# New places for the background pieces among TensorE's products in a two-layer hybrid decoder

## The chip, the cores and the metric

The kernel runs on one core of a Trainium2 chip. The metric is the device time of one execution in microseconds (us), the median of several runs. Five engines work side by side, each through its own instructions in their order: TensorE (PE; its weight loads are listed apart as PEld), VectorE (DVE), ScalarE (ACT), GpSimd (POOL) and SyncE (SP), which issues most of the DMA transfers. A result of one engine that another needs is passed on by a semaphore, and the engine that needs it stops its whole queue until it is there.

## The reference

Two DeepNorm layers over 256 tokens of width 1024, all in float32. Each layer has a mixer and a feed-forward part, and both are steered by shifts, scales and gates computed from a conditioning vector.

```python
mod = silu(c) @ w_cond[l] + b_cond[l]           # six rows of 1024
z = (x * (1 + sc1) + sh1) @ w_in[l]             # u_ssm, q, k, v, q_idx, k_idx, w_idx, g_ssm, g_attn
y_ssm  = glu(s5_scan(u_ssm))                    # 32 groups, 64 complex states, associative scan
y_attn = sparse_attention(rope(q), rope(k), v, top 64 keys by the indexer)
h = (sigmoid(g_ssm) * (y_ssm @ p_ssm) + sigmoid(g_attn) * (y_attn @ p_attn)) @ w_out
x = layer_norm(alpha * x + (1 + gt1) * h)
x = layer_norm(alpha * x + (1 + gt2) * swiglu_ffn(x * (1 + sc2) + sh2))
```

## The kernel before

Every float32 weight is read once from memory in pieces (`raw`, 512 KB) and split in two: ACT rounds it to a short type (`hi`, line 387) and DVE subtracts to get the remainder (`lo`, line 388). A product is then three matmuls: hi with the activation's hi, lo with hi, hi with lo. SP issues the next piece of weights when the split of an earlier one has freed its buffer, so the weights run some pieces ahead of the products.

The products are cut into **blocks**, in this order for a layer: u, qa and qb (query, indexer), kv, q0, q1 (`run_block`, line 1391, the activations moving), gs0 and gs1 (gate of the scan branch), the GLU, ga0 and ga1, ps, pa, wo (`run_cols`, line 1471, the weights stationary), then the feed-forward blocks. In layer 0 the blocks u, qa, qb are done by `run_first` (line 1542), whose activations (`MT`, line 1514) wait for the conditioning columns (lines 447, 451, 1511, 1512).

All else that TensorE does is **pieces** of background tasks: the scan's tables (`ssm_prep`, `ssm_tables`: lines 573 to 716), the scan (`ssm_run`: 847 the inputs, 860 and 861 transposes ahead of the scan, 885 and 889 the outputs, 909 transposes to the GLU), the indexer (`ev_idx_hi`, `ev_idx_lo`: rope at 964 to 968, transposes at 994 and 1013, scores at 1035), keys, values and queries (`ev_kv`, `ev_q`: 1068, 1081) and attention (`attend`: 1104, 1130, 1137). A task is a generator. After each group of products, a block calls `pump`, which lets every running task take a step. A task's `yield` says how many calls pass before its next step, and the table PACE overrides that number by the task's name, which start of it this is, and which yield:

```python
    r = next(self.gen, -1)
    if r != -1 and r != 0:
        self.i += 1
        r = PACE.get((self.name, self.n, self.i), r or 1)
    self.wait = max(r, 1) - 1
```

TensorE's order is thus written out by blocks and PACE. At a few points a block needs a task's result, and then the task is stepped to its end on the spot (`finish`): the scan before the GLU, attention before pa. The order of DVE, ACT, POOL and SP is set when the kernel is built, by a scheduler that places each instruction where it expects its operands.

A piece writes to PSUM through a tile `bk`, of which there are three in turn. A piece whose turn comes waits until DVE or ACT has read the tile three turns back. A block's sums are in tiles `acc`, two for each block, which the next block but one takes up again after DVE has read them.

Of the kernel before, what the change touches and what calls it, by code (L numbers as in the profile page):

```python
# [68 lines left out]


PACE = {
    ("after_prep", 0, 1): 1, ("after_prep", 0, 2): 1, ("after_prep", 0, 5): 1, ("after_prep", 0, 6): 1,
# [4 lines left out]
    ("attend", 0, 17): 2, ("attend", 0, 18): 1, ("attend", 0, 19): 1, ("attend", 0, 20): 4, ("attend", 0, 21): 4,
    ("attend", 0, 23): 1, ("attend", 0, 24): 1, ("attend", 0, 25): 1, ("attend", 1, 1): 2, ("attend", 1, 2): 2,
    ("attend", 1, 3): 2, ("attend", 1, 4): 3, ("attend", 1, 5): 3, ("attend", 1, 6): 3, ("attend", 1, 7): 2,
    ("attend", 1, 8): 2, ("attend", 1, 9): 3, ("attend", 1, 10): 2, ("attend", 1, 11): 2, ("attend", 1, 12): 3,  # L80
    ("attend", 1, 13): 3, ("attend", 1, 14): 3, ("attend", 1, 15): 3, ("attend", 1, 16): 2, ("attend", 1, 17): 3,
    ("attend", 1, 18): 1, ("attend", 1, 19): 1, ("attend", 1, 20): 3, ("attend", 1, 21): 3, ("attend", 1, 22): 2,
    ("attend", 1, 23): 4, ("attend", 1, 24): 4, ("attend", 1, 25): 6, ("cond_end", 0, 1): 5, ("cond_end", 0, 2): 4,
    ("cond_end", 0, 3): 2, ("cond_end", 1, 1): 3, ("cond_end", 1, 2): 5, ("cond_end", 1, 3): 1,
    ("cond_end", 2, 3): 2, ("cond_end", 3, 1): 5, ("cond_end", 3, 2): 4, ("cond_end", 3, 3): 4,
    ("cond_end", 4, 1): 4, ("cond_end", 4, 2): 6, ("cond_end", 4, 3): 3, ("cond_end", 5, 2): 4,
    ("cond_end", 5, 3): 3, ("cond_end", 6, 2): 4, ("cond_end", 6, 3): 1, ("end", 0, 1): 3, ("end", 0, 2): 3,
    ("end", 1, 1): 6, ("end", 1, 2): 8, ("ev_gate", 1, 1): 3, ("ev_gate", 2, 1): 1, ("ev_gate", 3, 1): 1,
    ("ev_gate", 4, 1): 6, ("ev_gate", 5, 1): 2, ("ev_gate", 6, 1): 1, ("ev_gate", 7, 1): 1, ("ev_idx_hi", 0, 3): 1,
    ("ev_idx_lo", 0, 1): 3, ("ev_idx_lo", 0, 3): 3, ("ev_idx_lo", 0, 4): 2, ("ev_idx_lo", 0, 5): 1,  # L90
    ("ev_idx_lo", 0, 8): 1, ("ev_idx_lo", 0, 9): 2, ("ev_idx_lo", 0, 10): 2, ("ev_idx_lo", 0, 11): 1,
    ("ev_idx_lo", 0, 12): 3, ("ev_idx_lo", 0, 13): 2, ("ev_idx_lo", 0, 15): 2, ("ev_idx_lo", 0, 16): 2,
    ("ev_idx_lo", 0, 17): 2, ("ev_idx_lo", 0, 19): 1, ("ev_idx_lo", 1, 1): 5, ("ev_idx_lo", 1, 2): 2,
    ("ev_idx_lo", 1, 4): 1, ("ev_idx_lo", 1, 5): 1, ("ev_idx_lo", 1, 6): 1, ("ev_idx_lo", 1, 9): 1,
    ("ev_idx_lo", 1, 10): 1, ("ev_idx_lo", 1, 11): 1, ("ev_idx_lo", 1, 12): 2, ("ev_idx_lo", 1, 13): 1,
    ("ev_idx_lo", 1, 14): 1, ("ev_idx_lo", 1, 15): 1, ("ev_idx_lo", 1, 16): 2, ("ev_idx_lo", 1, 18): 2,
# [1725 lines left out]
```

## Time and profile before

| | |
|---|---|
| three runs | 935.63 us median (933.08 to 936.72) |
| the profiled execution | 932.16 us, its span 930.4 us |
| PE busy | 878.5 us (94%) |
| DVE busy | 679.9 us (73%) |
| ACT busy | 406.0 us (44%) |
| POOL busy | 63.2 us (7%) |
| mean granted TensorE clock | 0.985 |

The span is from the first to the last instruction; the profiled execution's own time is 1.76 us longer. PE is busy nearly all the time, so what can be saved without touching the matmuls is in its idle time and in stretches at a lower granted clock. An engine's share of the whole span says little about a stretch: DVE is at 73% over all, and fuller in the mixers.

### The profile page before, as it was taken

The page shows a single profiled execution, that of the slowest core. Times are in us where ns is not written, and L with a number is a line of the kernel's source. Part 1 is how long each engine was busy: PE and PEld are TensorE (multiplying, and loading weights), DVE is VectorE, ACT ScalarE, POOL GpSimd, SP SyncE. Part 2 cuts the span into 40 slices and gives each one's busy share as a digit, 9 for nine tenths or more (in the row PEclk, how much of TensorE's full clock was granted, in tenths as well). Part 3 has the DMA queues.
Part 4 walks back from the last instruction along what each step waited for, and adds up shares of the span by engine and source line. Part 5 has one row for each costly group of instructions (what it writes and reads, how often), then busy time and mean ns, then how long its engine had stood idle before and what let it go on. Part 6 is the DMA issues. An engine that isn't in the chain of part 4 may idle for free.

```text
span 930.4 us, 16050 instructions
## 1 busy us (share of the span) xinstructions
PE 878.5 (94%) x6295; PEld 739.9 (80%) x6295; DVE 679.9 (73%) x1189; ACT 406.0 (44%) x597; POOL 63.2 (7%) x129
## 2 busy tenths in 40 slices
PE   6799799899998999999999979899999999999994
PEld 4457667788875799998886867699988799999894
DVE  5598799846677588867767988995659775656473
ACT  3034325744445353444344533566435544444340
POOL 4001610000000000000000360000000000000001
PEclk9899899999999999999999999999999999999998
DMA  9965988678786577777767698576737275655531
GB/s 292 318 226 131 226 239 272 227 252 258 247 264 232 177 244 264 259 263 245 237 213 226 179 225 287 187 220 205 227 114 260 99 271 176 190 183 183 182 113 45
DMA packets 105239, 201.37 MB, mean 216 GB/s; under 512 B 9688, under 2 KB 32964, under 8 KB 105164
## 3 DMA queue, kind: packets, MB, share of 16 engines
q1 hardware_dynamic: 100284, 191.81, 64.3%
q0 software_dynamic: 3008, 6.53, 3.3%
q10 hardware_dynamic: 1872, 2.01, 0.8%
q8 instruction: 49, 0.80, 0.3%
q14 instruction: 26, 0.21, 0.1%
HBM read 195.65 MB, written 2.05 MB: 212 GB/s over the span
## 4 chain that ended last, share of the span: by engine, by line
PE 58%; DVE 18%; DMA 14%; issue 5%; ACT 3%; SPq 0%; POOL 0%; POOLq 0%; DVEq 0%; ACTq 0%
PE acc L1471 34%; PE acc L1391 13%; DMA raw<-in_w_in_dram 5%; DVE lo L388 4%; PE cnd L475 3%; DMA raw<-in_w_cond_dram 2%; PE acc L1542 2%; ACT hi L387 1%; DMA raw<-in_w_down_dram 1%; DMA raw<-in_w_out_dram 1%; PE bk L1137 1%; PE bk L1104 1%; DMA raw<-in_w_gate_up_dram 1%; DVE sco L1043 1%; DVE tmp L965 1%
## 5 line engine op out<-in xcount | busy, mean ns | idle before, releaser
L388 DVE TENSOR_TENSOR lo<-raw,hi 128x1024 fp32r<-128x1024 f32 (+2 forms) x217 | 261.6, 1211 | 152.0 <-ACT hi L387 151.7
L387 ACT CAST hi<-raw 128x1024 fp32r<-128x1024 f32 (+2 forms) x217 | 224.9, 1042 | 316.3 <-PE acc L1471 110.9
L1471 PE MATMUL acc<-aTh,hi 128*128 128x256 f32 x832 | 137.4, 287 | 0.0
L1471 PE MATMUL acc<-aTl,hi 128*128 128x256 f32 x832 | 132.4, 281 | 0.0
L1471 PE MATMUL acc<-aTh,lo 128*128 128x256 f32 x832 | 132.4, 281 | 0.0
L1471 PEld LDWEIGHTS acc<-aTh,hi 128*128 128x128 f32 x832 | 113.2, 189 | 17.6 <-issue 13.9
L1471 PEld LDWEIGHTS acc<-aTl,hi 128*128 128x128 f32 x832 | 113.0, 188 | 0.0
L1471 PEld LDWEIGHTS acc<-aTh,lo 128*128 128x128 f32 x832 | 113.0, 188 | 0.0
L1391 PE MATMUL acc<-hi,aTh 128*128 128x512 f32 (+2 forms) x200 | 63.6, 403 | 4.0 <-DVE tmp L965 3.8
L1391 PE MATMUL acc<-lo,aTh 128*128 128x512 f32 (+2 forms) x200 | 60.1, 385 | 0.2 <-DVE lo L388 0.2
L1391 PE MATMUL acc<-hi,aTl 128*128 128x512 f32 (+2 forms) x200 | 59.8, 384 | 0.3 <-DVE aTl L1666 0.3
L1248 POOL TENSOR_TENSOR mv<-mv,mhalf 128x1 f32<-128x1 f32 x8 | 7.1, 894 | 621.9 <-DVE mv L1247 551.4
L1391 PEld LDWEIGHTS acc<-hi,aTh 128*128 128x128 f32 x200 | 34.1, 191 | 17.0 <-issue 7.5
L1391 PEld LDWEIGHTS acc<-hi,aTl 128*128 128x128 f32 x200 | 36.8, 190 | 8.8 <-DVE aTl L1666 0.8
L1391 PEld LDWEIGHTS acc<-lo,aTh 128*128 128x128 f32 x200 | 36.8, 191 | 8.5 <-DVE lo L388 1.0
L475 PE MATMUL cnd<-raw,csil 128*32 128x512 f32 x320 | 42.6, 605 | 0.0
L1391 PE MATMUL acc<-hi,MT 128*128 128x512 f32 (+1 forms) x144 | 36.9, 353 | 0.0
L1391 PE MATMUL acc<-lo,MT 128*128 128x512 f32 (+1 forms) x144 | 36.3, 349 | 0.0
L1391 PE MATMUL acc<-hi,q 128*128 128x512 f32 (+1 forms) x144 | 36.3, 349 | 0.0
L834 POOL DMA_DIRECT2D MT<-KT_d x64 | 33.8, 534 | 20.4 <-DMA MT<-KT_d 14.0
L1391 PEld LDWEIGHTS acc<-lo,MT 128*128 128x128 f32 x144 | 24.1, 188 | 4.0
L1391 PEld LDWEIGHTS acc<-hi,MT 128*128 128x128 f32 x144 | 23.8, 188 | 4.3 <-issue 0.8
(389 smaller groups left out, 1433.1 us busy)
## 6 DMA issues: line engine op xcount, KB each, us to landing
raw<-in_w_cond_dram SPq DMA_DIRECT2D x96, 512.0 KB
raw<-in_w_gate_up_dram SPq DMA_DIRECT2D x88, 512.0 KB
raw<-in_w_in_dram SPq DMA_DIRECT2D x62, 512.0 KB
raw<-in_w_down_dram SPq DMA_DIRECT2D x43, 512.0 KB
raw<-in_p_attn_dram SPq DMA_DIRECT2D x16, 512.0 KB
raw<-in_w_out_dram SPq DMA_DIRECT2D x16, 512.0 KB
MT<-KT_d POOLq DMA_DIRECT2D x64, 64.0 KB, 5.9
raw<-in_p_ssm_dram SPq DMA_DIRECT2D x16, 256.0 KB
```

What stands on the lines that cost most here:

```text
L387: i = A.copy(hv, ch.rv)
L388: j = place("lo", ch.lo_on).tensor_tensor(lv, ch.rv, hv.bitcast(F32), ALU.subtract)
L475: PE.matmul(acc[32 * g:32 * g + 32, 0:w], csil[:, kt], rv[:, w * (g % per):w * (g % per) + w], start=kt == 0, stop=kt == KD - 1, tile_posi ...
L834: P.dma_start(MT[16 * s:16 * s + 16, :, k], bass.AP(tensor=KT_d.tensor, offset=KT_d.offset + k * 16 * 1920 + 16 * s, ap=[[1920, 16], [240, ...
L965: V.tensor_tensor(w.rearrange("p (h a d) -> p h a d", a=2, d=half), src[:, :, ::-1], sn, ALU.mult)
L1043: V.scalar_tensor_tensor(sco, rels[:, o, nk * i:nk * i + nk], wi[:, t, h:h + 1], sco, ALU.mult, ALU.add)
L1104: PE.matmul(p[:, nk * (h - h0):nk * (h - h0) + nk], X["qT"][:, 4 * kv + h, 128 * t:128 * t + 128], X["kT"][:, kv, 0:nk], start=True, stop= ...
L1137: PE.matmul(p, X["V"][:, s, 128 * kv:128 * kv + 128], PT[:, s].rearrange("p h q -> p (h q)"), start=s == 0, stop=s == t)
L1248: root[0] = P.tensor_tensor(mv[:, 1:2], mv[:, 2:3], mhalf, ALU.pow)
L1391: PE.matmul(o, st_of(kt, t)[part == 2], (ch.lv if part == 1 else ch.hv)[:, k, :], start=kt == blk.first and part == 0, stop=kt == blk.last ...
L1471: PE.matmul(acc[:, 256 * i:256 * i + 256], w[:, k, n:n + 128], mov(kt)[part == 2], start=kt == blk.first and part == 0 and i == 0, stop=kt ...
L1542: PE.matmul(ac[t][:, 0:blk.n], AT32[:, t, kt], ch.rv[:, k], start=kt == 0 and (i < 2 or t == 0), stop=kt == KD - 1, skip_group_check=i == 2)
```

## The change

Only the table PACE differs. It has new numbers for entries that were there, and entries for yields that had none (the yield's own number counted there); four entries are for a task `taps_in`, a name that no generator in the kernel has. No instruction is added, removed or moved to another engine. Line numbers behind the table are 8 higher in the changed kernel, so line 1391 becomes 1399. Two lines of the table, before and after:

```diff
-    ("ssm_tables", 0, 2): 1, ("ssm_tables", 0, 3): 1, ("ssm_tables", 0, 4): 3, ("ssm_tables", 0, 5): 2,
-    ("ssm_tables", 0, 10): 2, ("turn", 0, 1): 6, ("turn", 0, 2): 3, ("turn", 1, 1): 3, ("turn", 1, 2): 3,
+    ('ssm_tables', 0, 1): 1, ('ssm_tables', 0, 2): 1, ('ssm_tables', 0, 3): 6, ('ssm_tables', 0, 4): 1,
+    ('ssm_tables', 0, 9): 1, ('ssm_tables', 0, 10): 7, ('taps_in', 1, 2): 1, ('taps_in', 1, 3): 3,
```

**Place 1, DVE at the start.** The end of the first table piece and the first activations in DVE's order; 587 (then 595) reads the transposes of line 573, 700 (708) makes four table tiles `E`, and 1512 and 1514 (1520, 1522) make the columns and the first activations `MT` for TensorE's first products. Before:

```order
L665 TENSOR_TENSOR p_55_249<-c_20_105,sp_269 128x512
L1512 TENSOR_TENSOR affs_139<-bk_230,bT_79 128x2
L1514 TENSOR_SCALAR MT_83<-q_35_138,affs_139 128x2x128
L552 COPY c_19_101<-c_19_101 4x128
L587 TENSOR_SCALAR p_55_249<-bk_250,K_1_68 128x512
L700 TENSOR_TENSOR E_388<-p_55_249,sp_269 128x1024 x4
```

And now:

```order
L673 TENSOR_TENSOR p_46_211<-c_20_105,sp_262 128x512
L595 TENSOR_SCALAR p_46_211<-bk_212,K_1_68 128x512
L708 TENSOR_TENSOR E_386<-p_46_211,sp_262 128x1024 x4
L560 COPY c_19_101<-c_19_101 4x128
L1520 TENSOR_TENSOR affs_139<-bk_243,bT_79 128x2
L1522 TENSOR_SCALAR MT_83<-q_35_138,affs_139 128x2x128
```

The transposes of line 573 are now on TensorE ahead of the first columns, and with them the four `E` operations have moved ahead of the first activations.

**Place 2, TensorE in the mixer of layer 0, blocks q0 and q1.** Line 847 makes the scan's inputs, line 1035 the first index scores (eight matmuls in turn, of which two are shown). Before, in q0:

```order
L1391 MATMUL acc_837<-hi_922,aTl_82 128x512 x2
L847 MATMUL bk_995<-BT_389,p_170_854 32x128 x16
L847 MATMUL bk_1014<-BT_389,p_170_854 32x128 x16
L1035 MATMUL bk_1036<-kiT_629,q_131_630 128x128
L1035 MATMUL bk_1037<-kiT_629,q_131_630 128x128
```

And now, in q1:

```order
L1043 MATMUL bk_1043<-kiT_623,q_130_624 128x128
L1399 MATMUL acc_1024<-hi_1011,aTh_81 128x512 x2
L1399 MATMUL acc_1024<-lo_1012,aTh_81 128x512 x2
L1399 MATMUL acc_1024<-hi_1011,aTl_82 128x512 x2
L855 MATMUL bk_1072<-BT_387,p_174_862 32x128 x16
L855 MATMUL bk_1091<-BT_387,p_174_862 32x128 x16
L1399 MATMUL acc_1023<-hi_1015,aTh_81 128x512 x2
```

The scores no longer stand right behind the scan's inputs; they come first, a group of products stands between, and both are a block later. The transposes 860 and 861 that followed before block q1 follow later too.

**Place 3, TensorE and DVE in the mixer of layer 1, start of block kv.** On TensorE before (the first row is the end of block qb, `acc_5553` is kv's first sum):

```order
L1391 MATMUL acc_5374<-hi_5354,aTl_82 128x256 x4
L847 MATMUL bk_5515<-BT_3611,p_844_5432 32x128 x16
L847 MATMUL bk_5534<-BT_3611,p_844_5432 32x128 x16
L1391 MATMUL acc_5553<-hi_5375,aTh_81 128x512 x2
L1391 MATMUL acc_5553<-lo_5376,aTh_81 128x512 x2
L1391 MATMUL acc_5553<-hi_5375,aTl_82 128x512 x2
L860 MATMUL bk_5561<-K_1_68,s_852_5513 128x128
```

And now:

```order
L1399 MATMUL acc_5357<-hi_5328,aTl_82 128x256 x4
L1399 MATMUL acc_5475<-hi_5358,aTh_81 128x512 x2
L1399 MATMUL acc_5475<-lo_5359,aTh_81 128x512 x2
L1399 MATMUL acc_5475<-hi_5358,aTl_82 128x512 x2
L1002 MATMUL bk_5483<-K_1_68,rope_5396 128x128 x2
```

The scan's inputs (847) and transposes (860, 861) have left this place for the middle and the end of kv. kv's first sum takes over the tile that DVE frees by its line 965 (`acc_5236` below, `acc_5220` in the changed kernel). On DVE before, up to that release:

```order
L971 TENSOR_TENSOR kid_5397<-tmp_5398,tmp_5399 128x128
L388 TENSOR_TENSOR lo_5634<-raw_5322,hi_5633 128x1024
L780 TENSOR_TENSOR c_799_5139<-c_799_5139,sp_5250 128x32x8
L781 TENSOR_TENSOR c_800_5140<-c_800_5140,sp_5250 128x32x8
L965 TENSOR_TENSOR tmp_5404<-acc_5236,K_69 128x256
```

And now:

```order
L979 TENSOR_TENSOR kid_5390<-tmp_5391,tmp_5392 128x128
L787 TENSOR_TENSOR c_800_5140<-c_799_5139,tw_5142 128x32x16
L784 TENSOR_TENSOR sp_5287<-c_800_5140,tw_5142 128x512
L396 TENSOR_TENSOR lo_5518<-raw_5332,hi_5517 128x1024
L785 TENSOR_TENSOR c_799_5139<-c_799_5139,tw_5142 128x32x16
L786 TENSOR_TENSOR sp_5287<-c_800_5140,tw_5142 128x512
L973 TENSOR_TENSOR tmp_5397<-acc_5220,K_69 128x256
```

Four table operations of 512 columns and a weight split that came behind the release before (lines 776 to 779 and 388) now come ahead of it. In return, lines 862 and 863 of the scan, which stood between it and the release of kv's second sum, are gone from here.

## Rows read from the trace of the kernel before

**Rows 1.** Waits of PE: what waited for whom, us in total, times, longest.

```profile
PE acc L1542 <- DVE MT L1514: 3.0, 3, 1.6
PE bk L909 <- DVE p L899: 2.6, 2, 1.7
PE bk L909 <- ACT sp L1038: 1.4, 1, 1.4
PE acc L1391 <- DVE lo L388: 0.2, 1, 0.2
```

**Rows 2.** Stretches: length, busy us by engine, granted clock, DMA share, GB/s.

```profile
31.68:38.51 6.83, 5.07 (x20) 1.58 (x20) 0.69 (x1) 1.10 (x2) 0.00 (x0) 0.50 1.10 348
...
76.00:106.78 30.78, 28.66 (x250) 21.78 (x248) 27.36 (x94) 12.45 (x19) 12.19 (x25) 1.00 0.79 197
106.78:113.60 6.82, 4.20 (x19) 3.59 (x20) 3.77 (x7) 0.77 (x1) 4.21 (x8) 0.50 1.02 229
113.60:176.00 62.40, 57.50 (x503) 45.03 (x503) 56.38 (x118) 30.16 (x41) 4.71 (x10) 1.00 0.75 235
...
537.00:547.10 10.10, 4.92 (x82) 3.98 (x81) 10.10 (x22) 3.65 (x7) 4.70 (x9) 1.00 1.05 237
547.10:550.51 3.41, 3.29 (x9) 2.60 (x10) 3.38 (x7) 0.32 (x1) 2.09 (x5) 0.50 0.82 150
550.51:600.00 49.49, 47.02 (x350) 33.47 (x352) 42.63 (x91) 20.68 (x30) 5.96 (x14) 1.00 0.74 230
```

**Rows 3.** Timeline of PE at the start: start, us, operation, [idle before].

```profile
21.02 3.78 PE L1542 MATMUL acc<-hi,MT 128*128 128x512 f32 x4 [0.70 <-DVE MT L1514]
...
28.11 1.07 PE L447 MATMUL bk<-raw,csil 128*32 128x256 f32 x16
33.01 1.08 PE L447 MATMUL bk<-raw,csil 128*32 128x256 f32 x8 [3.83 <-DMA raw<-in_w_cond_dram]
...
35.53 3.45 PE L1542 MATMUL acc<-hi,MT 128*128 128x512 f32 x4
```

**Rows 4.** Timeline of DVE at the start.

```profile
20.55 0.41 DVE L1514 TENSOR_SCALAR MT<-q,affs 128x256 f32<-128x256 f32 x1
...
25.36 0.75 DVE L587 TENSOR_SCALAR p<-bk,K 128x512 f32<-128x512 f32 x1 [4.24 <-PE bk L573]
26.15 4.63 DVE L700 TENSOR_TENSOR E<-p,sp 128x1024 f32<-128x1024 f32 x4
```

**Rows 5.** Timeline of PE in layer 0, block q0.

```profile
102.28 1.95 PE L847 MATMUL bk<-BT,p 128*32 128x128 f32 x64
...
109.40 2.08 PE L1035 MATMUL bk<-kiT,q 64*128 64x128 f32 x14 [4.75 <-DVE k L226]
```

**Rows 6.** Timeline of DVE there: the copy that the scores wait for.

```profile
108.67 0.68 DVE L226 COPY k<-bk 128x512 f32<-128x512 f32 x1
```

**Rows 7.** Timeline of PE in layer 1, block kv.

```profile
537.00 1.95 PE L847 MATMUL bk<-BT,p 128*32 128x128 f32 x64
...
540.37 0.27 PE L860 MATMUL bk<-K,s 128*128 128x128 f32 x1
...
541.13 0.27 PE L861 MATMUL bk<-K,s 128*128 128x128 f32 x1
...
547.22 1.22 PE L1391 MATMUL acc<-hi,aTh 128*128 128x512 f32 x2 [3.78 <-DVE tmp L965]
...
551.34 0.72 PE L1391 MATMUL acc<-hi,aTh 128*128 128x512 f32 x2
```

**Rows 8.** Timeline of DVE there, around the two releases.

```profile
538.36 0.42 DVE L965 TENSOR_TENSOR tmp<-acc,K 128x256 f32<-128x256 f32 x1
...
538.83 1.21 DVE L388 TENSOR_TENSOR lo<-raw,hi 128x1024 fp32r<-128x1024 f32 x1
...
546.16 0.67 DVE L863 TENSOR_TENSOR s<-c,bk 128x512 f32<-128x512 f32 x1
546.76 0.74 DVE L965 TENSOR_TENSOR tmp<-acc,K 128x256 f32<-128x256 f32 x2
```

More of the change, by code (lines that the diff above doesn't have):

```diff
@@ L77 @@
[L77 to L96, printed above, removed]
@@ new lines @@
+    ('attend', 0, 7): 3, ('attend', 0, 8): 1, ('attend', 0, 9): 1, ('attend', 0, 10): 3, ('attend', 0, 11): 2,
+    ('attend', 0, 12): 1, ('attend', 0, 13): 2, ('attend', 0, 14): 1, ('attend', 0, 15): 1, ('attend', 0, 16): 1,
+    ('attend', 0, 17): 1, ('attend', 0, 18): 3, ('attend', 0, 19): 1, ('attend', 0, 20): 4, ('attend', 0, 21): 4,
+    ('attend', 0, 23): 1, ('attend', 0, 24): 1, ('attend', 0, 25): 4, ('attend', 1, 1): 1, ('attend', 1, 2): 2,
+    ('attend', 1, 3): 2, ('attend', 1, 4): 3, ('attend', 1, 5): 3, ('attend', 1, 6): 2, ('attend', 1, 7): 2,
@@ new lines @@
+    ('cond_end', 2, 3): 2, ('cond_end', 3, 1): 2, ('cond_end', 3, 2): 4, ('cond_end', 3, 3): 4, ('cond_end', 4, 1): 4,
+    ('cond_end', 4, 2): 6, ('cond_end', 4, 3): 3, ('cond_end', 5, 2): 4, ('cond_end', 5, 3): 3, ('cond_end', 6, 2): 4,
+    ('cond_end', 6, 3): 1, ('end', 0, 1): 3, ('end', 0, 2): 3, ('end', 1, 1): 6, ('end', 1, 2): 10,
+    ('ev_gate', 1, 1): 2, ('ev_gate', 2, 1): 2, ('ev_gate', 3, 1): 1, ('ev_gate', 4, 1): 10, ('ev_gate', 5, 1): 2,
+    ('ev_gate', 6, 1): 1, ('ev_gate', 7, 1): 1, ('ev_idx_hi', 0, 1): 5, ('ev_idx_hi', 0, 2): 1,
@@ new lines @@
+    ('ev_idx_hi', 0, 3): 1, ('ev_idx_hi', 1, 3): 3, ('ev_idx_lo', 0, 1): 3, ('ev_idx_lo', 0, 3): 5,
+    ('ev_idx_lo', 0, 4): 3, ('ev_idx_lo', 0, 5): 1, ('ev_idx_lo', 0, 7): 2, ('ev_idx_lo', 0, 8): 2,
+    ('ev_idx_lo', 0, 9): 1, ('ev_idx_lo', 0, 10): 2, ('ev_idx_lo', 0, 11): 1, ('ev_idx_lo', 0, 12): 1,
+    ('ev_idx_lo', 0, 13): 1, ('ev_idx_lo', 0, 15): 5, ('ev_idx_lo', 0, 16): 1, ('ev_idx_lo', 0, 17): 1,
+    ('ev_idx_lo', 0, 18): 1, ('ev_idx_lo', 0, 19): 2, ('ev_idx_lo', 1, 1): 2, ('ev_idx_lo', 1, 2): 1,
@@ new lines @@
+    ('ev_idx_lo', 1, 4): 5, ('ev_idx_lo', 1, 5): 1, ('ev_idx_lo', 1, 6): 1, ('ev_idx_lo', 1, 7): 1,
+    ('ev_idx_lo', 1, 9): 1, ('ev_idx_lo', 1, 10): 4, ('ev_idx_lo', 1, 11): 1, ('ev_idx_lo', 1, 12): 2,
+    ('ev_idx_lo', 1, 13): 1, ('ev_idx_lo', 1, 14): 1, ('ev_idx_lo', 1, 15): 2, ('ev_idx_lo', 1, 16): 1,
+    ('ev_idx_lo', 1, 18): 1, ('ev_idx_lo', 1, 19): 1, ('ev_kv', 0, 1): 7, ('ev_kv', 0, 2): 1, ('ev_kv', 1, 1): 4,
+    ('ev_kv', 1, 2): 3, ('ev_q', 0, 1): 3, ('ev_q', 0, 2): 7, ('ev_q', 0, 3): 2, ('ev_q', 1, 1): 2, ('ev_q', 1, 2): 6,
@@ new lines @@
+    ('ev_q', 2, 1): 5, ('ev_q', 2, 2): 3, ('ev_q', 2, 3): 1, ('ev_q', 3, 1): 3, ('ev_q', 3, 2): 5,
+    ('ffn_cols', 0, 3): 3, ('ffn_cols', 0, 4): 1, ('ffn_cols', 1, 4): 1, ('ffn_cols', 2, 2): 1, ('ffn_cols', 3, 4): 4,
+    ('ffn_cols', 5, 2): 1, ('ffn_cols', 6, 2): 2, ('ffn_cols', 6, 3): 1, ('ffn_cols', 7, 1): 3, ('ffn_cols', 7, 4): 1,
+    ('ffn_cols', 8, 4): 3, ('ffn_cols', 9, 2): 4, ('ffn_end', 0, 1): 1, ('ffn_end', 0, 2): 4, ('ffn_end', 0, 3): 4,
+    ('ffn_end', 0, 4): 1, ('ffn_end', 1, 1): 2, ('ffn_end', 1, 2): 3, ('ffn_end', 1, 3): 1, ('ffn_end', 2, 3): 2,
@@ new lines @@
+    ('ffn_end', 2, 4): 1, ('ffn_end', 3, 1): 2, ('ffn_end', 3, 3): 2, ('ffn_end', 4, 1): 1, ('ffn_end', 4, 2): 2,
+    ('ffn_end', 4, 3): 2, ('ffn_end', 4, 4): 1, ('ffn_end', 5, 1): 1, ('ffn_end', 5, 2): 4, ('ffn_end', 5, 3): 4,
+    ('ffn_end', 5, 4): 3, ('ffn_end', 6, 1): 1, ('ffn_end', 6, 2): 3, ('ffn_end', 6, 3): 2, ('ffn_end', 6, 4): 1,
+    ('ffn_end', 7, 1): 6, ('ffn_end', 7, 2): 3, ('ffn_end', 7, 3): 5, ('ffn_end', 7, 4): 6, ('ffn_end', 8, 1): 2,
+    ('ffn_end', 8, 2): 4, ('ffn_end', 8, 3): 3, ('ffn_end', 8, 4): 1, ('ffn_end', 9, 1): 2, ('ffn_end', 9, 2): 7,
@@ new lines @@
+    ('ffn_gate', 7, 2): 2, ('ffn_gate', 8, 1): 2, ('ffn_gate', 8, 2): 1, ('ffn_gate', 9, 1): 2, ('ffn_gate', 9, 2): 2,
+    ('ffn_gate', 10, 1): 3, ('ffn_gate', 10, 2): 2, ('ffn_gate', 11, 1): 1, ('ffn_gate', 11, 2): 1,
+    ('first_bias', 0, 1): 20, ('first_bias', 0, 2): 1, ('merge_a', 1, 1): 1, ('merge_a', 1, 2): 1,
+    ('merge_a', 1, 3): 2, ('merge_a', 2, 3): 1, ('merge_a', 3, 1): 1, ('merge_a', 3, 3): 4, ('merge_s', 0, 1): 4,
+    ('merge_s', 1, 1): 3, ('merge_s', 2, 1): 2, ('ssm_prep', 0, 1): 1, ('ssm_prep', 0, 2): 1, ('ssm_prep', 0, 4): 1,
@@ new lines @@
+    ('ssm_prep', 0, 5): 1, ('ssm_prep', 0, 8): 1, ('ssm_prep', 0, 9): 1, ('ssm_prep', 0, 11): 2,
+    ('ssm_prep', 0, 12): 2, ('ssm_prep', 0, 13): 2, ('ssm_prep', 0, 14): 1, ('ssm_prep', 0, 16): 1,
+    ('ssm_prep', 0, 17): 1, ('ssm_prep', 0, 18): 1, ('ssm_prep', 0, 20): 1, ('ssm_prep', 0, 21): 1,
+    ('ssm_prep', 0, 22): 1, ('ssm_prep', 0, 24): 1, ('ssm_prep', 0, 26): 1, ('ssm_prep', 1, 1): 16,
+    ('ssm_prep', 1, 2): 2, ('ssm_prep', 1, 3): 4, ('ssm_prep', 1, 4): 6, ('ssm_prep', 1, 5): 8, ('ssm_prep', 1, 6): 7,
@@ new lines @@
+    ('ssm_prep', 1, 7): 3, ('ssm_prep', 1, 8): 2, ('ssm_prep', 1, 9): 4, ('ssm_prep', 1, 11): 6,
+    ('ssm_prep', 1, 12): 5, ('ssm_prep', 1, 13): 2, ('ssm_prep', 1, 14): 2, ('ssm_prep', 1, 15): 5,
+    ('ssm_prep', 1, 16): 6, ('ssm_prep', 1, 18): 1, ('ssm_prep', 1, 19): 5, ('ssm_prep', 1, 22): 6,
+    ('ssm_prep', 1, 23): 6, ('ssm_prep', 1, 24): 3, ('ssm_prep', 1, 26): 10, ('ssm_prep', 1, 27): 1,
+    ('ssm_prep', 1, 28): 1, ('ssm_run', 0, 2): 1, ('ssm_run', 0, 3): 4, ('ssm_run', 0, 4): 4, ('ssm_run', 0, 5): 3,
```

57 lines of the change are left out of this document (20 added, 37 removed).

## The prediction

> **What bounds the kernel now.** I read the busy times first: TensorE is busy for 878.5 of 930.4 us, and the change leaves all its matmuls in place. So only its idle time can be won, and time lost at a lower clock. Next I read who TensorE waits for, and took out what the change can reach: waits for DVE (or ACT) of pieces and first products in the two mixers and at the start [rows 1, 5, 7]. The layer norms and the tail keep their waits. Then I cut the mixers into stretches where the granted clock changes [rows 2].
>
> In layer 0, from 76 to 176 us, TensorE is idle for 30.78 - 28.66 = 2.1, 6.82 - 4.20 = 2.6 and 62.40 - 57.50 = 4.9 us, 9.6 together. 4.75 of that is one wait: the first index scores need a `bk` tile back, and the copy that frees it ends on DVE at 109.35 [rows 5, 6]. The middle stretch is at 0.50 of the clock (1.2 GHz, else 2.4), so half of its 4.20 busy us are lost too: 2.1. Without all this, the 100 us would be 88.3.
>
> In layer 1, from 537 to 600 us, the idle time is 5.2 + 0.1 + 2.5 us and the stretch at half clock costs 1.6 [rows 2]. The big wait is kv's second sum: its tile comes free when DVE has done line 965, 3.78 us late [rows 7]. 2.3 of the last 2.5 us are two waits of the transposes of line 909 (1.4, and the smaller of two that make 2.6) [rows 1].
>
> DVE is what TensorE waits for, and it is nearly full there: 87.5 of 100 us in layer 0, 10.10 of 10.10 us in front of the late release in layer 1 [rows 2]. In both places it works, in its order, on something that nobody waits for yet. That can be cured by order alone. At the start TensorE also waits for DVE: 3.0 us for the first activations in three waits, 0.7 of it ahead of the very first product [rows 1, 3].
>
> **The change, part by part.**
>
> *Start.* Line 587 and the four table operations of line 700 now come ahead of the first activations on DVE. They take 30.78 - 25.36 = 5.4 us [rows 4], so the first products start at about 26 instead of 21.0. Those products and what came with them lasted until 28.11, 7.1 us, so they now end at about 33. TensorE stopped there anyway: the next columns waited until 33.01 for weights from memory [rows 3]. That transfer is the work that hides the delay; if it hides nothing the cost is the full 5. What may come back: the stretch behind it was at half clock (0.50 from 31.68 to 38.51 [rows 2]); four products at 35.53 took 3.45 us, half of it too much, 1.7. If TensorE works from 26 to 33 without a stop it may find the full clock there. And DVE, idle for 4.24 us ahead of line 587 [rows 4], has these 5.4 us behind it, so the two later waits for activations, 3.0 - 0.7 = 2.3 us, should go. Bounds: 4.0 gained; 3 lost, if the first products run wholly at half clock and end near 36. I take 2.5 gained, nearer the upper end, since the transfer covers nearly all of the delay.
>
> *Layer 0.* The scan's inputs and first transposes stand later by a block, the scores come ahead of the scan's inputs. The queue that made 4.75 us is thus entered later, when DVE has done the table operations. No DVE instruction goes away, but adding up DVE's rows in both orders, 4.8 us of them move from ahead of the GLU's last operand to behind it. So DVE has 87.5 - 4.8 = 82.7 us to do in that stretch, TensorE 88.3. If DVE never starves, TensorE sets the time: 11.7 us gained. If DVE is filled only as it was, to 87.5%, it needs 82.7 / 0.875 = 94.5 us: 5.5 gained. DVE's idle time has two sources, one being TensorE's own stops (3.0 of 6.8 us in the half-clock stretch), and these shrink; so between the two: 8 gained, with small waits left at the new places of 860 and 909.
>
> *Layer 1, kv.* Here the order gives and takes. Ahead of the release of kv's first sum, DVE has four operations of 512 columns more (0.60 each, as from 546.16 to 546.76) and one split more (1.1, from 538.83 on): 3.5 us [rows 8]. That release came at 538.78; it will come at 542.3. TensorE, which has no scan inputs to do first, is there at 537.0 [rows 7]: a new wait of 5.3 us. Behind it on TensorE stands everything. The second release loses lines 862 and 863 and a third small one ahead of it, 0.6 + 0.6 + 0.3, and comes at 545.7 instead of 547.2, where TensorE took the tile up [rows 7]. To the end of this place (551.34) I count 1.5 us less for the release, 1.6 if the clock stays up, and 0.9 for transposes that went elsewhere: 547.3. But what went elsewhere must be done later, where TensorE has no idle time: 1.9 for line 847, and twice 0.9 for 860 and 861 (540.37 to 541.3) [rows 7]. That is 551.0, a gain of 0.3; at half clock again, a loss of 1.3. I take a loss of 0.5: the largest wait of this mixer is not cured but moved ahead by one group.
>
> *Layer 1, 909.* The transposes of 909 now stand some 18 us later in TensorE's own work, the DVE operation they wait for has only about 9 us more ahead of it (the sum of DVE's rows). Both waits should go: 2.3 gained. Layer 1 together: 1.8.
>
> The granted clock decides part of that. After the 4.75 us wait it was 0.50, after the 3.78 us wait too [rows 2]. The Trainium skill, "TensorE: Matmul & The Clock Gate", section "HAM oscillation — how this bites in real kernels", states that idle gaps send the engine back to half rate, and that the work behind them pays. By that rule, on which the trace agrees, the new wait of 5.3 us brings the half clock back, and the sum would be 0.8 us less.
>
> *Attention, feed-forward.* Attention's late pieces of layer 0 are pushed together right ahead of block pa0. That may cost a copy's wait; layer 1 has the same stack today and none of the waits at the rows of 1104, 1130 or 1137. Between 0 and 2 us, I take 0.5 lost. The table pieces for layer 1 move 5 to 17 us later among feed-forward products, where TensorE hardly waits for DVE; their work is the same, and I cost them at nothing, hidden by those products; without that cover each would cost its copy, 0.6 to 0.7 us.
>
> **Sum.** 2.5 + 8 + 1.8 - 0.5 = 11.8 us. The profiled execution has 932.16, so 920.4. The median of the runs is 3.5 above that execution, which gives 923.9; I say 924.
>
> **The rivals.**
>
> *The waits only move.* DVE is the bound in both mixers and a place further on takes each wait over. For it: layer 1's kv, worked out above, does just that. Against: in layer 0 DVE has less to do than TensorE. With DVE filled to 85%, layer 0 gives 2.7, layer 1 1.0, the start 0: 3.7 us, 932.
>
> *The half clock comes back* at both new stops, ahead of the first product at 26 and at kv. The first products then end 3 us later than without it, which takes the start's 2.5 and 0.7 more; layer 1 gives 1.0 instead of 1.8: 924 + 3.2 + 0.8 = 928. For it: both long waits of today were followed by it.
>
> *All is won.* Start 4.0, layer 0 11.7, layer 1 4.1 (full clock, small waits gone too): 19.8 us, 916.
>
> *Slower: late splits.* The scan's operations, moved back, stand on DVE among the splits of the weights (line 388, 1.2 us each). TensorE's waits for splits are 0.2 us in the whole run [rows 1], so the splits have a lead. It decides from the point where DVE falls behind the products by more than that lead: then every further us on DVE is one on TensorE, and SP, which asks for new weights when a split is done, falls behind with it. To end slower it must eat the 11.8 us and 4.7 more, some 14 splits without cover: 941. Against: DVE's work does not grow, and idle time is left to it in both mixers [rows 2].
>
> **Chances.** Forecast 0.53, waits move 0.17, half clock 0.12, all won 0.10, late splits 0.08. Runs of one kernel differ by some 0.4%, so less than 0.5% (4.7 us) can't be told from no change. Faster by more: 0.53 + 0.12 + 0.10 = 0.75; within: 0.17; slower: 0.08. The range reaches from 914, below the case in which all is won, to 936, above the case in which the waits move. The forecast's own range is 918 to 930.
>
> **What would show it.** In the changed kernel's trace: the first product at about 26 and the products behind the second columns at full clock; no wait of several us at the scores (1043 there), and no half clock near 107; at kv of layer 1 a wait of about 5 us for line 973 ahead of the first sum, a smaller one ahead of the second, and the clock behind it; no wait at 917. DVE over 90% busy from 76 us to the GLU. I am wrong if the waits of DVE in layer 0 add up to more than 6 us, if the first columns' weights come later because TensorE read the earlier ones later, or if `lo` shows up among TensorE's releasers.

## The result and the profile after

The changed kernel took 926.1 us median (923.5 to 926.5, four runs) where the kernel before took 936.2 us beside it: a ratio of 0.9884, 95% interval [0.9846, 0.9921]. Timed a second time it took 922.9 us, a ratio of 0.9867 [0.9841, 0.9892]. So 10 to 13 us are gone, more than 0.5%; 924 had been forecast. The profiled execution took 926.43 us, its span 924.6.

TensorE has the same work as before; its idle time has shrunk. From the page of the changed kernel, the busy times:

```profile
PE 877.5 (95%) x6295; PEld 743.2 (80%) x6295; DVE 680.6 (74%) x1189; ACT 406.5 (44%) x597; POOL 64.5 (7%) x129
```

The waits of PE of the changed kernel (what waited for whom, us in total, times, longest; its line numbers are 8 higher than those of before from line 140 on):

```profile
PE acc L1550 <- DVE MT L1522: 6.4, 2, 4.7
PE acc L1399 <- DVE tmp L972: 5.5, 1, 5.5
PE bk L869 <- ACT s L234: 4.4, 1, 4.4
...
PE bk L855 <- ACT sp L1046: 1.9, 1, 1.9
...
PE bk L1021 <- ACT p L234: 1.6, 1, 1.6
...
PE acc L1399 <- DVE lo L396: 0.2, 1, 0.2
```

Read against [rows 1, 5, 7]: the 4.75 us wait of the scores and the waits of 909 (now 917) are gone, DVE no longer stands in a row of layer 0's mixer, but three new rows name ACT there, 1.9 + 4.4 + 1.6 = 7.9 us. The wait ahead of the first product has grown from 0.7 to 4.7 us, as the change asks.

Timeline of PE in the changed kernel, at the three places of [rows 3, 5, 7] (start, us, operation, idle before in brackets):

```profile
26.01 3.71 PE L1550 MATMUL acc<-hi,MT 128*128 128x512 f32 x4 [4.68 <-DVE MT L1522]
...
34.59 0.64 PE L455 MATMUL bk<-raw,csil 128*32 128x256 f32 x8 [0.81 <-DMA raw<-in_w_cond_dram]
35.16 1.98 PE L1550 MATMUL acc<-hi,MT 128*128 128x512 f32 x4
...
107.94 1.16 PE L1043 MATMUL bk<-kiT,q 64*128 64x128 f32 x16
...
113.60 1.08 PE L855 MATMUL bk<-BT,p 128*32 128x128 f32 x32 [1.89 <-ACT sp L1046]
...
121.97 0.47 PE L869 MATMUL bk<-K,s 128*128 128x128 f32 x1 [4.40 <-ACT s L234]
...
537.83 1.19 PE L1399 MATMUL acc<-hi,aTh 128*128 128x512 f32 x2 [5.47 <-DVE tmp L972]
```

The second columns' wait for weights is 0.81 us where it was 3.83, and the four products behind it take 1.98 us where they took 3.45: the clock is whole there. The scores at 107.94 do not wait. The first sum of key and value in layer 1 waits 5.47 us. Stretches of the changed kernel (length, busy us by engine, granted clock, DMA share, GB/s):

```profile
76.00:100.00 24.00, 22.42 (x161) 16.69 (x160) 21.01 (x79) 10.06 (x16) 9.82 (x20) 0.95 0.76 197
100.00:125.00 25.00, 18.71 (x141) 13.58 (x141) 18.09 (x32) 6.06 (x9) 9.78 (x19) 0.84 0.89 223
125.00:174.00 49.00, 48.17 (x459) 39.09 (x458) 44.23 (x96) 25.92 (x33) 0.13 (x1) 1.00 0.71 228
...
107.00:110.60 3.60, 3.60 (x27) 2.50 (x25) 2.56 (x4) 1.84 (x3) 2.84 (x6) 1.00 1.04 266
113.60:117.60 4.00, 3.97 (x39) 2.68 (x39) 3.12 (x6) 0.44 (x1) 1.66 (x3) 0.66 1.06 217
117.60:122.00 4.40, 0.03 (x1) 0.03 (x1) 1.02 (x1) 2.02 (x3) 0.00 (x0) 0.89 0.58 155
122.00:125.00 3.00, 3.00 (x11) 2.71 (x12) 2.51 (x6) 0.00 (x0) 0.13 (x1) 0.50 0.44 147
537.80:540.50 2.70, 2.67 (x6) 2.04 (x7) 2.70 (x8) 0.00 (x0) 1.96 (x4) 0.50 1.04 240
```

Against [rows 2]: the half clock has gone from 107 and come back behind the new waits, at 122 and at 537.8 (0.50, which is 1.2 GHz). DVE's work from 76 us to the GLU is 21.01 + 18.09 + 44.23 = 83.3 us, forecast 82.7; but these lie in 98 us, 85%. From 117.6 to 122.0 it is busy 1.02 of 4.40 us, and PE not at all. DVE is not what bounds this place any more. Timeline of ACT there:

```profile
119.90 1.04 ACT L395 CAST hi<-raw 128x1024 fp32r<-128x1024 f32 x1 [5.86 <-DMA raw<-in_w_in_dram]
120.85 0.58 ACT L234 COPY k<-bk 128x512 f32<-128x512 f32 x1
121.33 0.59 ACT L234 COPY s<-bk 128x512 f32<-128x512 f32 x1
```

The copy that line 869 waits for is the third row: half a microsecond of work, behind a cast of weights that stood 5.86 us waiting for memory. In ACT's queue the copy comes after that cast, so the piece is as late as the weights are. The trace of before held the same pair:

```profile
112.83 1.05 ACT L387 CAST hi<-raw 128x1024 fp32r<-128x1024 f32 x1 [7.89 <-DMA raw<-in_w_in_dram]
...
113.78 0.58 ACT L226 COPY s<-bk 128x512 f32<-128x512 f32 x1
```

There TensorE, late by its wait of 4.75 us for DVE, came to the transposes of line 860 at 115.29, when the copy was done. What else moved through the DMA engines then is in their queues from 100 to 125 us (packets, MB, share of the 16 engines):

```profile
q1 hardware_dynamic: 1653, 4.15, 63.2%
q0 software_dynamic: 690, 1.41, 25.3%
```

q0 is POOL's queue: the gathers of the scan's table `MT` (line 842; 32 of 64 KB each, issued from 90 to 116.5 us). That they are what makes the weights late is tested below.

To see where each us comes and goes I lined up the foreground products of two traces, which are the same in every version, and subtracted the start of each. How much later (+) or earlier (-) than in the profile of before a version stands, in us:

| at, in the profile of before | 78.2 kv of layer 0 | 143.6 | 174.4 GLU | 491.1 layer 1 | 551.3 past kv | 686.1 | end |
|---|---|---|---|---|---|---|---|
| before, a second profile | +1.5 | +1.0 | +1.8 | +3.9 | +6.2 | +7.2 | +7.9 |
| changed | -4.0 | -0.7 | -2.3 | -3.5 | -8.2 | -6.3 | -5.7 |
| changed, second | -4.2 | -2.9 | -5.3 | -5.7 | -10.5 | -10.6 | -9.5 |
| start alone | -3.8 | -1.2 | +2.1 | +3.2 | +5.9 | +6.8 | +7.2 |
| layer 0 alone | -0.1 | +9.1 | +2.5 | +1.4 | +3.7 | +4.8 | +5.9 |
| the rest alone | +0.9 | -0.4 | +1.6 | +0.1 | -3.3 | -3.4 | -3.1 |
| all but layer 0 | -5.3 | -3.1 | -0.9 | +1.0 | -2.9 | -3.0 | -2.7 |
| old mixer, layer 1 | -2.0 | +1.4 | -0.5 | -0.5 | -1.9 | -0.9 | 0.0 |
| old feed-forward pieces | -4.0 | +0.6 | -1.9 | -3.6 | -6.4 | -5.9 | -4.6 |
| one plain load | -4.0 | -9.6 | -12.4 | -15.3 | -19.8 | -19.9 | -19.1 |
| gathers in pairs | -4.0 | -7.3 | +3.2 | +1.4 | -3.6 | +0.6 | +1.5 |
| first nine pairs | -3.7 | -3.7 | -4.6 | -6.1 | -9.8 | -10.0 | -8.7 |

Two profiles of one kernel differ by some 2 us in a stage, 3 to 4 in layer 1; a smaller difference in one trace means nothing.

### The profile page after: what moved, and what is told of

Read it like the earlier page. It is cut to its first block, busy times and chain, and to the rows that moved or that the text cites. A ratio compares the mean times of both kernels' runs of the same rounds, so it can differ in the third digit from the quotient of the medians.

```text
span 924.6 us, 16033 instructions
## 1 busy us (share of the span) xinstructions
PE 877.5 (95%) x6295; PEld 743.2 (80%) x6295; DVE 680.6 (74%) x1189; ACT 406.5 (44%) x597; POOL 64.5 (7%) x129
## 4 chain that ended last, share of the span: by engine, by line
PE 69%; DMA 13%; DVE 8%; issue 4%; ACT 2%; SPq 2%; POOL 1%; POOLq 0%; ACTq 0%; DVEq 0%
PE acc L1479 38%; PE acc L1399 18%; DMA raw<-in_w_in_dram 4%; PE cnd L483 3%; DMA MT<-KT_d 3%; DVE lo L396 2%; SPq L358 2%; DMA raw<-in_w_gate_up_dram 2%; PE acc L1550 1%; DMA raw<-in_w_out_dram 1%; PE bk L1112 1%; DMA lo<-in_w_in_dram 1%; PE bk L1145 1%; ACT hi L395 1%; DMA raw<-in_w_cond_dram 1%
## 5 line engine op out<-in xcount | busy, mean ns | idle before, releaser
L1399 PEld LDWEIGHTS acc<-hi,q 128*128 128x128 f32 x144 | 24.1, 188 | 3.9
```

The source lines that it names most:

```text
L1399: PE.matmul(o, st_of(kt, t)[part == 2], (ch.lv if part == 1 else ch.hv)[:, k, :], start=kt == blk.first and part == 0, stop=kt == blk.last ...
```

## The experiments

**Which part of the table is worth what.** Four mixes of the old and the new numbers: six entries that belong to the start, 40 to layer 0's mixer, and 79 others. For example

```diff
-    ("first_bias", 0, 1): 17,                         # start
+    ("first_bias", 0, 1): 20,
-    ("ssm_run", 0, 10): 7, ("ssm_run", 0, 13): 5,     # layer 0
+    ('ssm_run', 0, 10): 1, ('ssm_run', 0, 13): 4,
-    ("ssm_run", 1, 11): 1, ("ssm_prep", 1, 1): 12,    # rest
+    ('ssm_run', 1, 11): 4, ('ssm_prep', 1, 1): 16,
```

Start alone. 

> The new numbers for the first tables and the first columns alone; the mixers as before. Both theories agree: the start gives back 2.5 us (the prediction's term) to 3.5 us (what the changed kernel's trace shows where the first products end), so about 0.3% faster, 932.5 to 933.5 where the kernel before has 936.

Layer 0 alone. 

> The new numbers for layer 0's mixer alone. The prediction's term: DVE is what TensorE waits for, 8 us faster, about 928. The rival, read from the changed kernel's trace: TensorE's waits there have only passed from DVE's copies to ACT's copies, which stand behind weight casts that wait for memory; no gain, or 1 us lost, 935 to 937.

The rest alone. 

> The new numbers for everything behind layer 0's mixer (second tables among the feed-forward products, layer 1). The prediction's term: 1.8 us faster, about 934, with a wait of about 5 us at kv of layer 1. The rival from the trace of the changed kernel: 4 to 5 us faster, 931 to 932, with the same wait.

All but layer 0. 

> All new numbers except those of layer 0's mixer, which are the old ones. The prediction's terms: 2.5 + 1.8 = 4.3 us faster than before, about 932, and so 6 us slower than the changed kernel (926). The rival: as fast as the changed kernel or 1 us faster, 925 to 927, with the old waits at the index scores.

Measured: start alone 939.4 us, 1.0018 [0.9993, 1.0043]; layer 0 alone 939.8, 1.0018 [1.0, 1.0036]; the rest alone 929.5, 0.9917 [0.9893, 0.9941]; all but layer 0 930.6, 0.9933 [0.9908, 0.9957]. So neither the start nor layer 0 is worth anything by itself, and two thirds of the gain lie in the rest. The start alone, slower than either theory had it, and the rest, faster than either, missed what was expected. The table says why the start is worth nothing alone: the first blocks end some 4 us earlier (column 78.2), and with the old places in layer 0 the mixer eats that and more (-3.8 becomes +2.1, -5.3 becomes -0.9). With the new places it eats little (-4.0 becomes -2.3). The rows name the same chain as above. In start alone TensorE's longest wait in this mixer is

```profile
112.56 1.93 PE L855 MATMUL bk<-BT,p 128*32 128x128 f32 x32 [8.51 <-ACT sp L1046]
```

and ACT's operation of line 1046 stands there behind two casts, the first of which waited 9.32 us for its weights. The new places of layer 0 are worth something only in that they keep the start's gain: with the start and the rest new, they are worth 5 to 6 us (0.9884 and 0.9867 against 0.9933).

**The same two kernels again.**

> The changed table once more, unchanged, for a narrower interval beside the parts: if the parts add up (start 0, layer 0 0, the rest 0.8% faster) it is 0.8% faster; if start and layer 0 help only together, 1.2% as first measured. Its second profile shows whether the waits of ACT's copies in layer 0 (1.9 and 4.4 us at 855 and 869) are there each time.

> The kernel before once more, for a second profile: its median is 936 to 937 but its profiled execution took 932. If this one takes 936 or more, its stages show which part varies; both theories leave that open, the layer 0 mixer (memory queue) being the likelier place.

The changed kernel gave 0.9867, as said above. The kernel before, one execution: 940.0 us, with its layer 1 3.4 us longer than in the profile that the prediction went by (+3.9 at 491 becomes +7.2 at 686). The profile that the prediction went by was a lucky one there: line 909, for one, waits 3.9 us for DVE in the second profile, 2.6 in the first [rows 1].

**Layer 1: the mixer or the feed-forward pieces.** The changed table with the old numbers for one or the other:

```diff
-    ('ssm_run', 1, 11): 4, ('ev_kv', 1, 1): 4,        # old mixer, layer 1
+    ('ssm_run', 1, 11): 1,
-    ('ssm_prep', 1, 1): 16, ('ffn_gate', 2, 2): 1,    # old feed-forward pieces
+    ('ssm_prep', 1, 1): 12, ('ffn_gate', 2, 2): 2,
```

Old mixer. 

> The changed table, but with the old numbers for the tasks of layer 1's mixer (tables, scan, indexer, attention pieces there); start, layer 0 and the pieces among the feed-forward products stay new. Theory: layer 1's gain of about 7 us lies in the mixer, at the scan's products of line 917 (in the shifted numbering) and ahead of key and value, so the time is 5 to 7 us over the changed kernel, a ratio to before of 0.992 to 0.996 (928.5 to 932). Rival: the gain lies in the pieces among the feed-forward products and the vector engine then arriving less late at layer 1's layer norm and u block; then this kernel stays within 3 us of the changed one, 0.986 to 0.991.

Old feed-forward pieces. 

> The mirror of the run before: the changed table with the old numbers for the pieces among the feed-forward products (layer 1's scan tables, the column sums, the ends and turns), and the new ones for layer 1's mixer. Theory (mixer): 0 to 2 us over the changed kernel, ratio 0.986 to 0.990. Rival (feed-forward pieces): 4 us or more over it, 0.991 or above, with waits of 1.5 to 2 us back at the layer norm and the u block of layer 1 near 503 to 515 us.

Old mixer: 930.6 us, 0.9912 [0.988, 0.9945]. Old feed-forward pieces: 924.3 us, 0.9868 [0.9838, 0.9899], the time of the changed kernel. The mixer's places are likely what counts for the time, 3 to 4 us by these ratios, less than the 5 to 7 expected; the intervals overlap, so it is not shown. The waits of PE with the old mixer, which the changed kernel has not:

```profile
PE acc L1399 <- DVE tmp L973: 3.8, 2, 2.2
...
PE bk L1043 <- ACT sp L1046: 2.1, 1, 2.1
...
PE bk L917 <- ACT sp L1046: 1.6, 1, 1.6
...
PE bk L855 <- ACT p L234: 1.2, 1, 1.2
```

They add up to 8.7 us against the changed kernel's one wait of 5.5: the long new wait of kv is dearer than each of them and cheaper than all. With the old feed-forward pieces, a wait of layer 1's u block for `aTh` is back, the rival's sign, but no time that the runs can tell. In the kernel before, and in this run (in the changed kernel no wait for `aTh` is over 0.3 us):

```profile
507.81 0.73 PE L1391 MATMUL acc<-s,aTh 128*128 128x512 f32 x2 [1.97 <-ACT aTh L1192]
```

```profile
504.31 0.73 PE L1399 MATMUL acc<-s,aTh 128*128 128x512 f32 x2 [2.16 <-ACT aTh L1200]
```

**Layer 0 without the gathers.** In layer 0, `MT` is loaded in one piece of 2 MB of the input weights, so the scan's output is not computed there; layer 1 is unchanged.

```diff
+        if l == 0:
+            P.dma_start(MT.rearrange("p a b c -> p (a b c)"), w_in[l][0:128, 0:4096])
+        else:
```

> The changed table, and in layer 0 the 32 gathers of the scan's matrix MT (64 KB each, rows of 512 bytes) are replaced by one plain load of as many bytes from the input weights, so the scan's output is not computed. Theory: the gathers and the weights share a full memory queue from 95 to 120 us, weights land late, and ACT's copy of the scan's inputs stands behind the cast of such a weight; then the waits at 855 and 869 go and the GLU begins 5 to 8 us earlier, 5 to 8 us less than the changed kernel. Rival, the prediction's: DVE's order sets layer 0; then the time stays within 2 us of the changed kernel.

913.1 us, 0.9749 [0.9721, 0.9777], 10 to 13 us under the changed kernel where 5 to 8 were expected. Timeline of ACT, the same copy as above:

```profile
112.43 1.05 ACT L395 CAST hi<-raw 128x1024 fp32r<-128x1024 f32 x1 [1.54 <-DMA raw<-in_w_in_dram]
...
113.86 0.59 ACT L234 COPY s<-bk 128x512 f32<-128x512 f32 x1
```

and the waits of PE that stood at 7.9 us:

```profile
PE bk L858 <- ACT sp L1049: 1.1, 1, 1.1
PE bk L872 <- ACT s L234: 0.8, 1, 0.8
PE bk L1024 <- ACT p L234: 0.7, 1, 0.7
```

The cast waits 1.54 us instead of 5.86, the copy comes 7.5 us earlier, and the mixer from kv to the GLU gains 8.4 us where the changed kernel loses 1.7 in one profile and gains 1.1 in the other. The load does not depend on the scan's tables and goes out at 73.5 us, well ahead of that place; so the run shows what it is worth to have these 2 MB out of the 90 to 123 us, and says nothing about the form of their rows.

**Gathers through SP's queue,** in four groups six steps of `pump` apart:

```diff
+                    SP.dma_start(MT[16 * s:16 * s + 16, :, k],
...
+                yield 6
...
+        while not t_mt.done:
+            yield 0
```

> The changed table; the gathers of MT go through SP's queue in four groups, six pumps apart, between the weights, in both layers. If the gathers' crowd on the memory queue is what makes the weights late, the long waits of layer 0 shrink and it is 2 to 6 us faster than the changed kernel; layer 1's wait at kv (5.5 us, for DVE) stays. If DVE's order sets layer 0, no change; slower if SP, busy with the gathers' issues, asks for weights later.

957.2 us, 1.021 [1.0174, 1.0245], far slower. But the run does not test what it was meant to. With the last two lines the scan's outputs are held back until the last group has been issued, and so their place in TensorE's order changes too. The first of them in layer 0, in this run and in the changed kernel:

```profile
170.28 0.40 PE L900 MATMUL bk<-E,s 128*32 128x128 f32 x8
```

```profile
144.18 0.43 PE L893 MATMUL bk<-E,s 128*32 128x128 f32 x8
```

and waits of PE of this run:

```profile
PE bk L924 <- DVE p L914: 11.1, 2, 9.3
...
PE bk L874 <- ACT s L234: 3.5, 1, 3.5
```

The outputs now stand shortly ahead of the GLU, and what DVE makes of them is waited for there (9.3 us at 924). Lined up as in the table, this kernel is at +0.1 at 160.0 and at +13.2 at the GLU. The gathers of layer 0 went out from 89.0 to 119.7 us, hardly otherwise than from 90 to 116.5 in the changed kernel, so they were not spread, and the wait for the copy of `s` stayed (3.5 us at 874). What SP's queue is worth for the gathers is open.

**Gathers in pairs on POOL's queue.** Ahead of each pair POOL copies one element of the pair issued two pairs earlier into the next pair's place; the queue then holds at most four. Otherwise the work is that of the changed kernel.

```diff
+        pairs = [(32 * s, k) for k in range(4) for s in range(T // 2)]
+        for n, (a, k) in enumerate(pairs):
+            if n >= 2:
+                b, j = pairs[n - 2]
+                P.tensor_copy(MT[a:a + 32, 0, k, 0:1], MT[b:b + 32, 0, j, 0:1])
+            for s in (a // 16, a // 16 + 1):
                 P.dma_start(MT[16 * s:16 * s + 16, :, k],
```

> The changed kernel, with the 32 gathers of the scan's table MT held to four in flight: ahead of each pair of gathers GpSimd copies one element of the pair issued two pairs earlier into the place of the next pair, so that the queue waits for it. Everything else is unchanged. Theory (the burst of small-row gathers takes the memory queues from the weights of layer 0's mixer, and the scan's copies stand behind a cast that waits for those weights): the weight cast waits less, the products of lines 855, 869 and 1021 wait 2 to 6 us less together, and the time is 2 to 8 us under the changed kernel, a ratio to before of 0.979 to 0.986. Rival (what counts is the sum of bytes and rows, however they are spread): the same time within 2 us, 0.986 to 0.990. Second rival: the gathers end too late for the scan's products at 893 near 148 us, which then wait several us, or GpSimd's zeroing behind them comes late: 2 to 10 us over the changed kernel.

929.1 us, 0.9913 [0.9883, 0.9944]: 3 to 4 us slower than the changed kernel by the ratios, whose intervals overlap. The theory and its second rival are both in the trace. Timeline of PE:

```profile
112.94 1.94 PE L859 MATMUL bk<-BT,p 128*32 128x128 f32 x32 [2.81 <-ACT sp L1050]
...
149.02 0.39 PE L901 MATMUL bk<-MT,p 128*32 128x128 f32 x1 [10.78 <-DMA MT<-KT_d]
```

The wait of 4.4 us for the copy is gone. SP's requests for the input weights and ACT's casts of them match one to one in their order, so the weights of the cast ahead of that copy can be followed. SP asked for them in the changed kernel (the first of the two) at

```profile
109.30 5.11 SPq L358 DMA_DIRECT2D raw<-in_w_in_dram  x2
```

and in this run, with the cast:

```profile
108.63 5.11 SPq L358 DMA_DIRECT2D raw<-in_w_in_dram  x2
```

```profile
113.94 1.05 ACT L395 CAST hi<-raw 128x1024 fp32r<-128x1024 f32 x1 [0.56 <-DMA raw<-in_w_in_dram]
```

From request to cast it is 10.6 us in the changed kernel (8.9 in its second profile) and 5.3 us here; without gathers it was 6.3 (106.14 to 112.43). The weights are asked for at nearly the same time, and it is the transfer beside the burst that is slow. At 143.6 the kernel stands at -7.3 where the changed one stood at -0.7 and -2.9: what the gathers' burst takes from layer 0 comes back when it is spread, with the work whole. Then the scan waits 10.78 us for the last gathers, which POOL issued at 141.9.

**Only the first nine pairs, only in layer 0.**

```diff
-            if n >= 2:
+            if l == 0 and 2 <= n < 9:
```

> As the run that held the gathers to four in flight, but only in layer 0 and only for the first nine of the sixteen pairs: from the tenth pair on, which that run issued at 118.9 us, the queue fills as in the changed kernel, and layer 1 is as in the changed kernel. In that run the copy for line 869 no longer stood behind a cast that waits, and the foreground was 5 to 6 us ahead of the changed kernel from 124 to 144 us; then the scan's product waited 10.8 us for the last gathers, issued at 141.9. In the changed kernel 32 gathers go out in 27 us, so the last 14 should be out by some 131 and landed by some 138 us. Theory: the wait for MT falls under 3 us, most of the 5 us stays, and the time is 2 to 6 us under the changed kernel, a ratio to before of 0.981 to 0.986. Rival: the second half of the gathers then holds up the weights and the products behind 120 us instead, and the time stays within 2 us of the changed kernel, 0.986 to 0.990. Second rival: MT still comes several us late, 0.990 or above.

920.7 us beside 939.8 for before: 0.9799 [0.976, 0.9838], the fastest kernel of this study with the whole work in it. It was not timed beside the changed kernel; by the ratios it is 6 to 8 us better than that one, by the medians themselves 2 to 5. But it did not get there as I expected. Timeline of POOL:

```profile
90.42 4.21 POOL L846 DMA_DIRECT2D MT<-KT_d  x8 [2.06 <-DMA KT_d<-k]
...
97.37 3.74 POOL L846 DMA_DIRECT2D MT<-KT_d  x7 [1.38 <-DMA MT<-KT_d]
101.16 4.79 POOL L844 COPY MT<-MT 32x1 f32<-32x1 f32 x2
105.89 2.61 POOL L846 DMA_DIRECT2D MT<-KT_d  x5
...
121.48 0.13 POOL L888 MEMSET s<- 128x16 f32 x1 [7.85 <-PE bk L873]
122.01 1.05 POOL L846 DMA_DIRECT2D MT<-KT_d  x2 [0.40 <-POOL s L888]
```

The pairs that wait for nothing were put ahead of those that do, so 22 gathers go out at once, by 108.5; then POOL's zeroing of `s` waits for PE, and the other ten follow from 122 on. Between 108.5 and 122 no gather is issued. Timeline of ACT:

```profile
108.89 1.04 ACT L395 CAST hi<-raw 128x1024 fp32r<-128x1024 f32 x1 [8.13 <-DMA raw<-in_w_in_dram]
...
116.32 1.05 ACT L395 CAST hi<-raw 128x1024 fp32r<-128x1024 f32 x1 [0.36 <-DMA raw<-in_w_in_dram]
```

The cast ahead of the copy waits 0.36 us, and no wait for `MT` or for the copy of `s` is left in PE's rows. But the cast before it, behind the 22 gathers, waits 8.13 us, and TensorE's waits for ACT in this mixer add up to 8.0 us, as in the changed kernel (7.9). They stand at other places, 4.0 and 1.4 at 859, 1.5 at 897 and 1.1 at 1025; the longest:

```profile
PE bk L859 <- ACT sp L1050: 4.0, 1, 4.0
```

So the burst is moved here more than it is spread. In its profile, though, this kernel stands at or near the better of the changed one's two profiles (the table), and its profiled execution took 923.7 us, the slowest of its six. That it is faster than the changed kernel is likely from the timing; where, and why, its trace does not show.

## Why the prediction was right, and where it was not

The time (924 forecast, 926.1 and 922.9 measured), the range and the sign were right. Its sum was not, and that it came so near is in part luck: layer 0 was put 9 us too high, layer 1 and the start 4 and 2 too low. The 3.5 us from the profiled execution to the median did not carry over either: the changed kernel's two profiled executions, 926.43 and 922.65 us, are within 0.4 us of their medians, while the profile of before was a fast one, by 3.4 us in layer 1 alone. From the table, versions with the new numbers of a stage against those with the old ones:

- *Start, 2.5 gained (4.0 to -3).* Six traces with the new numbers stand at -3.8, -5.3, -4.0, -4.2, -2.0 and -4.0 at 78.2, four with the old ones at 0, +1.5, -0.1 and +0.9: 4.5 us gained, a little over the upper end. The steps held: the first product at 26.01, the transfer hid the delay, the clock was whole at 35.16. The first four products run at half clock (3.71 us), as before. Not as forecast: of the later waits for activations one of 1.7 us (at 58.6) stayed.
- *Layer 0, 8 gained: the step that failed.* From 78.2 to the GLU the kernels with the new start and the new places lose 1.7, gain 1.1, lose 1.5 and lose 2.1; those with neither lose 0, 0.3 and 0.7; those with the new start and the old places lose 5.9 and 4.4. The term is about -1 us, not +8, though without the new places it would have been some 4 us worse. The step said that DVE is the bound and shrinks by 4.8 us of work, so that the time follows its busy share. DVE did shrink as worked out (83.3 us) and the waits for it went; but behind it stood a chain that the trace of before also held, unread: ACT's copies behind casts that wait for memory, the memory shared with the gathers. In before it was hidden by the wait for DVE. The run without gathers moved this stretch by 7 to 10 us against the changed kernel with DVE's work unchanged (82.8 us from 76 to 164, 94% of it): with the gathers gone the stretch gains 8.4 us, about what the step had said. The run in pairs moved it by 5 to 7 up to 143.6. The sign for it was on the list, in part: DVE at 85%, not over 90%. The other sign, more than 6 us of waits for DVE, did not come: the 7.9 us were ACT's.
- *Layer 1, 1.8 gained.* From 491 to 686 four traces with the new numbers gain 2.8, 4.9, 3.5 and 4.0; with the old ones they show 0, +3.4, +3.6 and +3.4. That is 6 us. The kv step was right in place and size, a new wait of 5.5 us (5.3 forecast) with the half clock behind it, and the waits at 917 are gone as forecast. Two things were mis-sized. About 3 of the 6 us lie ahead of kv, in layer 1's first sums, which the prediction put at nothing with the pieces among the feed-forward products: lined up at 515.4 as well, the kernels with the new feed-forward pieces gain 1.3 to 1.5 us from 491, the wait of 1.97 us for `aTh` being gone; the old feed-forward run loses 0.4, and three traces with the old numbers lose 1.7 to 2.4. And the price of the old order was read from one profile in which its waits were short.
- *Attention and the rest, 0.5 lost.* From the GLU to 491 and from 686 to the end most versions differ by no more than some 2 us, as two profiles of one kernel do. The forecast can't be told from nothing.

Of the rivals, *the waits only move* came true in layer 0, in a form that I hadn't written (to ACT and the memory, not to the next place on DVE). *The half clock comes back* came true at kv, and at the start for the first four products only. *All is won* and *late splits* did not: splits cost PE 0.2 us, as before.

## What to carry to other kernels

When the engine that is waited for has been freed, ask what its own queue and its neighbour's wait for next: a copy of half a microsecond is as late as the cast ahead of it in the queue, and that cast as late as its weights. Test the parts of a schedule together as well as alone; here start and layer 0 cost nothing or a little alone and were worth some 4 us together. And size a term on two profiles of the kernel before, since one can be 3 us off in a single stage.

## What the runs showed of the hardware

Weights land late beside a burst of gathers. From SP's request to ACT's cast the same piece of 512 KB took 10.6 and 8.9 us in the two profiles of the changed kernel, 6.3 us without gathers in this mixer, and 5.3 with the gathers in pairs.

The gathers move rows of 512 bytes. In the changed kernel, from 100 to 125 us, a MB of theirs took 0.253 x 25 / 1.41 = 4.5 us of the 16 DMA engines, a MB of the weights 0.632 x 25 / 4.15 = 3.8 us, so a gather's MB cost 1.2 times a weight's. The same stretch gives 1.2 in the profile of before, and 1.3, 1.4 and 1.5 in the changed kernel's second profile, with pairs and with the first nine pairs. The Trainium skill, "DMA: Bandwidth & Descriptors", section "Specifications", puts the least size for line rate at 512 bytes. The traces agree only roughly: at that size a byte still cost 1.2 to 1.5 times as much as a weight's. That the timing of the gathers counts more than this price is what the run in pairs shows up to 143.6, with the same rows.
